# Tokens of k tiles 4 to 7 placed 128 bytes further on in their SBUF tile

## The chip, the cores and the metric

One Trainium2 chip; the kernel runs as one launch on one of its cores. The metric is the device time of that launch in microseconds. A run's time is compared with runs of the kernel before on the same chip.

## The reference

One layer of a bidirectional encoder on 256 tokens of width 2048, all in float32:

```python
h = rmsnorm(x)
q, k, v, u = split(h @ w_in)             # 1536 + 512 + 512 + 512 columns
a = rmsnorm(window_attention(q, k, v))   # 12 heads of 128, 4 kv heads, |t-s| <= 128, ALiBi, sink
f = rmsnorm(fourier_mix(u))              # per group: Re(DFT2 over positions and channels), a map
x = x + concat(a, f) @ w_out
gate, val = split(rmsnorm(x) @ w_up)     # 2 x 5504 columns
gate = depthwise_conv3(gate) + dw_b
x = x + (gelu(gate) * val) @ w_down
y = rmsnorm(x)
```

## The kernel before

**Numbers in two parts.** Each float32 matrix is split on the chip into a high part, which the reduced float32 type of TensorE (F32R) holds, and a low part, the rest. A product is three matmuls: high by high, high by low, low by high. ScalarE writes the high part (L170 for weights, L262 for tokens), VectorE subtracts to get the low one (L171, L263).

**The tokens.** Sixteen k tiles of 128 features each. Four SBUF tiles `hT0` to `hT3` hold four k tiles each; a k tile is 512 floats in every partition, 256 tokens of the high part and 256 of the low. So `hT1` holds k tiles 4 to 7. Behind the attention the same memory takes the normalised residual under the names `hU0` to `hU3` (`turn_x_out`).

**The weights.** They stream from HBM in units of 128 x 2048 floats (`raw`, three buffers) and are split into `parts` (three buffers of 2 x 2048 + 128 floats). `PLACES` says how many floats behind the start of its half each part begins: (0, 32) for "still", (16, 16) for "first", (0, 0) for "moving", (28, 28) for "product".

**Two kinds of matmul.** In `moving_weights` (L303 to L313) the tokens are the stationary operand and 512 columns of weights move: u, v, the output projection, late parts of the down projection. In `still_weights` (L315 to L325) a 128x128 block of weights is stationary and 256 tokens move; one tile of 128 output features takes 16 k tiles times three matmuls, 48 in all, all recorded under L322. There are 16 such tiles for q and k (`ps_q`, `ps_k`) and 86 for the up projection (`ps_gate`, `ps_val`), 102 together. Within a k tile the order is: high weights by high tokens, high weights by low tokens, low weights by high tokens.

**The order of the work.** It is written out by hand. u and v come first; then the q and k tiles, with the matmuls of attention and of the Fourier group put between them (`at(before, ...)`); then the output projection (L309 to L311); then the list of `ff_items`: gate and value tiles of features 0 to 7 back to back, then groups in which a product of the down projection (L1010 to L1012, 512 columns) stands behind every up tile but some, then late down products, the last six up tiles back to back, and the last down products. Each step splits the weights of the unit two ahead.

**The Fourier group.** After L505 ScalarE copies each of four groups out of PSUM into `yh` (L513, two buffers) and VectorE joins them into `y` (L518 to L522) one step later; the copy of the next group follows in the next step.

Of the kernel before, what the change touches and what calls it, by code (L numbers as in the profile page):

```python
# [8 lines left out]
F32 = mybir.dt.float32  # L9
F32R = mybir.dt.float32r  # L10
# [3 lines left out]
P = 128  # L14
D = 2048
S = 256
# [15 lines left out]
V_G1, V_G2, V_GA, V_GF, V_DW, V_DB, V_SINK = 0, 16, 32, 44, 48, 177, 220  # L32
# [15 lines left out]
N_U, N_V, N_QK = 0, 4, 8  # L48
# [35 lines left out]
def block_kernel(  # L84
# [21 lines left out]
    base = ctx.enter_context(tc.tile_pool(name="base", bufs=1))  # L106
# [4 lines left out]
    def f32(ap):  # L111
        return ap.bitcast(F32)

    def bank(pool, name):
        return pool.tile([P, 512], F32, tag=pool.name, name=name)


    units = [(w_in[i], 2048, "first" if i < N_QK else "still") for i in range(24)]
    units += [(w_out[i], 2048, "moving") for i in range(16)]
    n_front = len(units)  # L120
    items, up_index = ff_items(), {}
# [11 lines left out]
    raws, halves = {}, {}  # L133


    PLACES = {"still": (0, 32), "first": (16, 16), "moving": (0, 0), "product": (28, 28)}

    def parts_tile(name, place):
        t = wp.tile([P, 2 * 2048 + 128], F32R, tag="parts", name=name, bufs=3)
        oh, ol = PLACES[place]  # L140
        return t[:, oh : oh + 2048], t[:, 2048 + ol : 4096 + ol]

    def load(i, pieces=1):
        if i < len(units) and i not in raws:
            src, n, _ = units[i]
            raws[i] = wp.tile([P, 2048], F32, tag="raw", name=f"raw{i}", bufs=RAW)
            m = n // pieces
            for p in range(pieces):
                s = slice(p * m, (p + 1) * m)
                nc.sync.dma_start(raws[i][:, s], src[:, s])  # L150
                yield
# [28 lines left out]
    ph = pa.enter_context(tc.tile_pool(name="pa", bufs=1))  # L180

    hT = []
    vec = base.tile([P, V_N], F32, tag="vec", name="vec")
    xTc = [cat_pool.tile([P, 512], F32, tag="cat", name=f"xT{c}") for c in range(8)]
    chan = cat_pool.tile([P, 512], F32, tag="cat", name="chan")[:, 0 : 2 * P]
# [16 lines left out]
    first = load(0, 4)  # L202
# [50 lines left out]
    ps = bank(dn, "ps_warm")  # L253
# [3 lines left out]
    def vcol(o, n=1):  # L257
        return vec[:, o : o + n]

    def split_scaled(dst, src, g):  # L260

        nc.scalar.activation(dst[:, 0:S], src, AF.Copy, scale=g)  # L262
        nc.vector.scalar_tensor_tensor(  # L263
            dst[:, S : 2 * S], src, g, f32(dst[:, 0:S]), ALU.mult, ALU.subtract
        )
# [49 lines left out]
    def still_weights(hi, lo, ps, kk):  # L315


        for k in kk:
            h = hT[k // 4][:, k % 4, :]
            s = slice(k * P, (k + 1) * P)  # L320
            for n, (w, o) in enumerate([(hi, 0), (hi, S), (lo, 0)]):
                nc.tensor.matmul(  # L322
                    ps[:, 0:S], w[:, s], h[:, o : o + S],
                    start=k == 0 and n == 0, stop=k == NK - 1 and n == 2,
                )  # L325

    def hk(k):
        return hT[k // 4][:, k % 4, :]

    later = []  # L330

# [26 lines left out]


    for c in range(4):  # L360
        t = base.tile([P, 4, 512], F32R, tag=f"hT{c}", name=f"hT{c}")
        hT.append(t)
    ps_u = [bank(mm, f"ps_u{b}") for b in range(2)]
    for k in range(NK):
        c, q = k // 4, k % 4
        if q == 0:
            parts = split_parts(c, 4 if c < 2 else 2)
        split_scaled(hk(k), xTc[k // 2][:, (k % 2) * S : (k % 2 + 1) * S], vcol(V_G1 + k))
        next(parts, None)
        hi, lo = halves[c]  # L370
        for b in range(2):
            moving_weights(
                hi, lo, 512, [k], hk, b, ps_u[b], k == 0, k == NK - 1, q0=q
            )
        if q == 3:
            for _ in parts:
                pass
            del halves[c]
# [77 lines left out]
    held = {}  # L456
# [52 lines left out]


    def fourier_channels_copy(g):
        h = held["h", g] = ph.tile([P, S], F32, tag="tmp", name=f"yh{g}", bufs=2)
        nc.scalar.activation(h, held.pop(("y", g))[:, 0:S], AF.Copy)  # L513

    def fourier_channels_join(g):
# [30 lines left out]
    def fourier_channels_steps():  # L546
        for g in range(NG):
            i = 8 + g
            at(before, i, fourier_channels, g)
            at(beside, i, fourier_channels_copy, g)  # L550
            at(behind, i, fourier_channels_join, g)
            at(beside, i + 1, fourier_channels_out, g)
        at(before, 14, total, sq_f, "f")
        at(beside, 14, total_scale, "f", FW)
# [3 lines left out]
    for c in range(4):  # L558

        def work(hi, lo):  # L560
            for b in range(2):
                moving_weights(
                    hi, lo, 512, range(4 * c, 4 * c + 4), hk, b, ps_v[b], c == 0, c == 3
                )

        unit(N_V + c, work)
# [138 lines left out]
    for n, (kind, h) in enumerate(QK_ORDER):  # L705

        def work(hi, lo):
            ps = st["ps", kind, h] = bank(mm, f"ps_{kind}{h}")
            still_weights(hi, lo, ps, range(NK))

        unit(N_QK + n, work)
# [22 lines left out]
    def turn_x(c):  # L734
        turn_x_out(c, turn_x_in(c))
# [14 lines left out]
        return pss  # L750

    def turn_x_out(c, pss):
        t = base.tile([P, 4, 512], F32R, tag=f"hT{c}", name=f"hU{c}")
        for k4 in range(4):
            ps = pss[k4 // 2][:, k4 % 2 * S : (k4 % 2 + 1) * S]
            split_scaled(t[:, k4, :], ps, vcol(V_G2 + 4 * c + k4))
        hT2.append(t)

    at(before, N_OUT + 6, total, sq_a, "a")
# [2 lines left out]
    for n, (c, kq) in enumerate(OUT_ORDER):  # L762
        i = N_OUT + n

        def work(hi, lo):
            if kq == 0:
                ps_a[c] = [bank(mm, f"ps_a{c}{b}") for b in range(2)]
            if kq == 3:
                ps_a[c, "f"] = [bank(dn, f"ps_ff{c}{b}") for b in range(2)]
            ps = ps_a[c] if kq < 3 else ps_a[c, "f"]  # L770
            for b in range(2):
                moving_weights(
                    hi, lo, 512, range(4 * kq, 4 * kq + 4), cat.get, b, ps[b],
                    kq in (0, 3), kq in (2, 3),
                )

        unit(i, work)
        if kq >= 2:
            part = "a" if kq == 2 else "f"
            ps = ps_a[c] if kq < 3 else ps_a[c, "f"]  # L780
            last = c in added
            added.add(c)
            if n == len(OUT_ORDER) - 1:
                later.append(out_post(c, part, ps))
                continue

            at(behind if (c, kq) == (0, 2) else beside, i + 1, out_add, c, part, ps)
            if last:
                at(behind, i + 1, out_sums, c)
                at(before, i + 2, lambda c=c: st.update({("x", c): turn_x_in(c)}))  # L790
                at(beside, i + 2, lambda c=c: turn_x_out(c, st.pop(("x", c))))
# [180 lines left out]
    held = {(c, p): bank(dn, f"ps_{p}_{c}") for c in range(2) for p in ("P1", "N5")}  # L972
# [98 lines left out]
    for q in range(2):  # L1071
        kind, j = items[q]
        ps = bank(mm, f"ps_{kind}{j}")
        pair.append((ps, *halves.pop(n_front + q)))
        still_weights(*pair[q][1:], ps, range(12))
        if q == 0:
            ff_step(0)
            turn_x(3)
            hT[:] = hT2
    for ps, hi, lo in pair:  # L1080
        still_weights(hi, lo, ps, range(12, NK))
# [7 lines left out]
    for n, it in enumerate(items):  # L1089
# [8 lines left out]
        if it[0] in ("gate", "val"):  # L1098
            kind, j = it
            ps = bank(mm, f"ps_{kind}{j}")  # L1100
# [4 lines left out]
        if it[0] == "product":  # L1105
            kind, g, c, p = it
# [3 lines left out]
            else:  # L1110
                ps = bank(mm, f"ps_{p}{g}{c}")
# [4 lines left out]
        else:  # L1116
            kind, g, c = it
            hi, lo = halves.pop(up_index[n])
            ps = [bank(mm, f"ps_l{g}{c}{b}") for b in range(2)]
# [10 lines left out]
    i = up_index[n]  # L1130
# [145 lines left out]
```

## Time and profile before

| | |
|---|---|
| median of 3 runs | 959.62 us (959.04 to 959.85) |
| the profiled execution | 959.13 us, of which the span from first to last instruction 957.4 |
| TensorE, matmuls | 947.8 us busy, 99% of the span |
| TensorE, weight loads | 884.8 us, 92% |
| VectorE | 703.0 us, 73% |
| ScalarE | 510.5 us, 53% |
| HBM read | 208.65 MB, 220 GB/s over the span |
| mean granted TensorE clock | 0.997 |

How to read it: PE is a matmul, PEld a load of stationary weights, which overlaps it. Matmuls are pipelined, so the time of one (from its start to its end) is longer than the spacing of two. In the timeline, neighbours of one line and tile are merged into one row: start, time from the first start to the last end, count.

### The profile page before, as it was taken

The page shows a single profiled execution, that of the slowest core. Times are in us where ns is not written, and L with a number is a line of the kernel's source. Part 1 is how long each engine was busy: PE and PEld are TensorE (multiplying, and loading weights), DVE is VectorE, ACT ScalarE, POOL GpSimd, SP SyncE. Part 2 cuts the span into 40 slices and gives each one's busy share as a digit, 9 for nine tenths or more (in the row PEclk, how much of TensorE's full clock was granted, in tenths as well). Part 3 has the DMA queues.
Part 4 walks back from the last instruction along what each step waited for, and adds up shares of the span by engine and source line. Part 5 has one row for each costly group of instructions (what it writes and reads, how often), then busy time and mean ns, then how long its engine had stood idle before and what let it go on. Part 6 is the DMA issues. An engine that isn't in the chain of part 4 may idle for free.

```text
span 957.4 us, 15831 instructions
## 1 busy us (share of the span) xinstructions
PE 947.8 (99%) x6721; PEld 884.8 (92%) x6721; DVE 703.0 (73%) x822; ACT 510.5 (53%) x552; POOL 44.6 (5%) x59
## 2 busy tenths in 40 slices
PE   9999999999999999999999999999999999999996
PEld 7799999888899999999999999999999999998985
DVE  5658766666566667786888877987778879787664
ACT  6855655544453346555555555554555655553433
POOL 0000000000000000000000000000000000000003
PEclk9999999999999999999999999999999999999998
DMA  8954444455555676879688798777987786775542
GB/s 322 340 195 164 161 138 157 151 176 186 196 181 197 253 224 209 231 248 301 205 270 251 232 293 264 234 251 221 285 256 249 218 292 200 242 246 211 177 132 88
DMA packets 33558, 211.77 MB, mean 221 GB/s; under 512 B 3792, under 2 KB 4304, under 8 KB 9424
## 3 DMA queue, kind: packets, MB, share of 16 engines
q1 hardware_dynamic: 29744, 184.54, 52.8%
q0 software_dynamic: 3600, 26.22, 14.7%
q8 instruction: 52, 0.85, 0.3%
q14 instruction: 18, 0.15, 0.1%
q10 hardware_dynamic: 144, 0.01, 0.0%
HBM read 208.65 MB, written 2.10 MB: 220 GB/s over the span
## 4 chain that ended last, share of the span: by engine, by line
PE 96%; DMA 2%; ACT 0%; DVE 0%; issue 0%; POOL 0%; ACTq 0%; POOLq 0%; SPq 0%
PE ps_gate L322 25%; PE ps_val L322 25%; PE ps_q L322 7%; PE ps_P L1010 3%; PE ps_P L1011 3%; PE ps_P L1012 3%; PE ps_k L322 2%; PE ps_a L311 2%; PE ps_a L309 2%; PE ps_a L310 2%; PE ps_N L1010 2%; PE ps_N L1012 2%; PE ps_N L1011 2%; DMA raw<-in_w_in 2%; PE ps_l L309 2%; PE ps_l L310 2%
## 5 line engine op out<-in xcount | busy, mean ns | idle before, releaser
L171 DVE TENSOR_TENSOR parts<-raw,parts 128x2048 fp32r<-128x2048 f32 (+3 forms) x145 | 313.1, 2159 | 76.7 <-ACT parts L170 76.3
L170 ACT ACTIVATE parts<-raw 128x2048 fp32r<-128x2048 f32 (+3 forms) x144 | 262.4, 1823 | 170.4 <-PE ps_val L322 40.0
L322 PEld LDWEIGHTS ps_gate<-hU,parts 128*128 128x128 f32 x2064 | 242.6, 188 | 2.3
L322 PE MATMUL ps_gate<-hU,parts 128*128 128x256 f32 x2064 | 244.5, 277 | 0.0
L322 PEld LDWEIGHTS ps_val<-hU,parts 128*128 128x128 f32 x2064 | 242.1, 188 | 2.2
L322 PE MATMUL ps_val<-hU,parts 128*128 128x256 f32 x2064 | 244.1, 277 | 0.0
L322 PE MATMUL ps_q<-hT,parts 128*128 128x256 f32 x576 | 69.5, 279 | 0.0
L322 PEld LDWEIGHTS ps_q<-hT,parts 128*128 128x128 f32 x576 | 67.9, 188 | 0.0
L1011 PE MATMUL ps_P<-parts_P,op_P 128*128 128x512 f32 x128 | 49.8, 389 | 0.0
L1010 PE MATMUL ps_P<-parts_P,op_P 128*128 128x512 f32 x128 | 49.8, 389 | 0.0
L1012 PE MATMUL ps_P<-parts_P,op_P 128*128 128x512 f32 x128 | 49.8, 389 | 0.0
L906 ACT ACTIVATE parts_N<-sumw 128x2048 fp32r<-128x2048 f32 x16 | 30.7, 1917 | 35.7 <-PE ps_val L322 22.5
L907 DVE TENSOR_TENSOR parts_N<-sumw,parts_N 128x2048 fp32r<-128x2048 f32 x16 | 36.6, 2289 | 16.8 <-ACT parts_N L906 16.8
L309 PE MATMUL ps_a<-parts,cat 128*128 128x512 f32 x96 | 37.9, 395 | 0.0
L311 PE MATMUL ps_a<-parts,cat 128*128 128x512 f32 x96 | 37.5, 390 | 0.0
L310 PE MATMUL ps_a<-parts,cat 128*128 128x512 f32 x96 | 37.3, 389 | 0.0
L1010 PE MATMUL ps_N<-parts_N,op_N 128*128 128x512 f32 x96 | 37.3, 389 | 0.0
L1011 PE MATMUL ps_N<-parts_N,op_N 128*128 128x512 f32 x96 | 37.3, 389 | 0.0
L1012 PE MATMUL ps_N<-parts_N,op_N 128*128 128x512 f32 x96 | 37.3, 389 | 0.0
L804 DVE TENSOR_TENSOR fa_g<-ps_gate,r2b 128x256 f32<-128x256 f32 x43 | 18.1, 422 | 23.1 <-PE ps_gate L322 23.1
L1012 PEld LDWEIGHTS ps_P<-parts_P,op_P 128*128 128x128 f32 x128 | 24.0, 188 | 5.0
L906 ACT ACTIVATE parts_P<-sumw 128x2048 fp32r<-128x2048 f32 x8 | 15.3, 1917 | 23.1 <-PE ps_gate L322 13.2
(307 smaller groups left out, 1267.3 us busy)
## 6 DMA issues: line engine op xcount, KB each, us to landing
raw<-in_w_up SPq DMA_DIRECT2D x86, 1024.0 KB, 5.4
raw<-in_w_in SPq DMA_DIRECT2D x21, 1024.0 KB, 4.9
raw<-in_w_out SPq DMA_DIRECT2D x16, 1024.0 KB, 4.8
sumw<-in_w_down POOLq DMA_DIRECT2D x16, 1024.0 KB, 8.8
raw<-in_w_down_late SPq DMA_DIRECT2D x8, 1024.0 KB, 5.0
raw<-in_w_down_last SPq DMA_DIRECT2D x4, 768.0 KB, 4.3
raw<-in_w_in SPq DMA_DIRECT2D x8, 256.0 KB, 6.2
xs<-in_x SPq DMA_DIRECT2D x4, 512.0 KB, 10.1
```

The lines of the kernel that those rows point to most:

```text
L170: nc.scalar.activation(hi[:, s], raw[:, s], AF.Copy)
L171: nc.vector.tensor_tensor(lo[:, s], raw[:, s], f32(hi[:, s]), ALU.subtract)
L309: nc.tensor.matmul(ps, ah, wh, start=first and q == q0, stop=False)
L310: nc.tensor.matmul(ps, al, wh, start=False, stop=False)
L311: nc.tensor.matmul(ps, ah, wl, start=False, stop=last and q == q0 + len(kk) - 1)
L322: nc.tensor.matmul(ps[:, 0:S], w[:, s], h[:, o : o + S], start=k == 0 and n == 0, stop=k == NK - 1 and n == 2,)
L804: nc.vector.tensor_tensor(add, ps[:, 0:S], r2b, ALU.mult)
L906: nc.scalar.activation(hi, src, AF.Copy)
L907: nc.vector.tensor_tensor(lo, src, f32(hi), ALU.subtract)
L1010: nc.tensor.matmul(ps, o[:, 0, p, :], hi[:, s], start=first and p == 0, stop=False)
L1011: nc.tensor.matmul(ps, o[:, 1, p, :], hi[:, s], start=False, stop=False)
L1012: nc.tensor.matmul(ps, o[:, 0, p, :], lo[:, s], start=False, stop=last and p == 3)
```

## The change

The tile of k tiles 4 to 7 gets 128 floats more, and its contents begin 32 floats (128 bytes) further on; this holds for `hT1` and for `hU1`. The weights of u and v that are multiplied with these k tiles (units 1 and 5) move from place (16, 16) to (48, 48), also 128 bytes further. The weights of all other stages stay where they were in their tiles, so that in the 102 tiles of `still_weights` tokens and weights stand otherwise to each other at k tiles 4 to 7 than at the other twelve. All tiles behind `hT1` in SBUF begin 512 bytes later. To make room, `yh` has one buffer instead of two.

```diff
-    units = [(w_in[i], 2048, "first" if i < N_QK else "still") for i in range(24)]
+    first = ["first", "first_off", "first", "first"] * 2
+    units = [(w_in[i], 2048, first[i] if i < N_QK else "still") for i in range(24)]
...
-    PLACES = {"still": (0, 32), "first": (16, 16), "moving": (0, 0), "product": (28, 28)}
+    PLACES = {"still": (0, 32), "first": (16, 16), "first_off": (48, 48), "moving": (0, 0), "product": (28, 28)}
...
+    def tokens_tile(c, name):
+        o = 32 if c == 1 else 0
+        n = 2048 + (128 if c == 1 else 0)
+        t = base.tile([P, n], F32R, tag=f"hT{c}", name=f"{name}{c}")
+        return [t[:, o + q * 512 : o + (q + 1) * 512] for q in range(4)]
...
-            h = hT[k // 4][:, k % 4, :]
+            h = hT[k // 4][k % 4]
...
-        t = base.tile([P, 4, 512], F32R, tag=f"hT{c}", name=f"hT{c}")
-        hT.append(t)
+        hT.append(tokens_tile(c, "hT"))
...
-        h = held["h", g] = ph.tile([P, S], F32, tag="tmp", name=f"yh{g}", bufs=2)
+        h = held["h", g] = ph.tile([P, S], F32, tag="tmp", name=f"yh{g}", bufs=1)
...
-        t = base.tile([P, 4, 512], F32R, tag=f"hT{c}", name=f"hU{c}")
+        t = tokens_tile(c, "hU")
...
-            split_scaled(t[:, k4, :], ps, vcol(V_G2 + 4 * c + k4))
+            split_scaled(t[k4], ps, vcol(V_G2 + 4 * c + k4))
```

More of the change, by code (lines that the diff above doesn't have):

```diff
@@ L327, in hk @@
     def hk(k):
-        return hT[k // 4][:, k % 4, :]
+        return hT[k // 4][k % 4]
     later = []
```

## Prediction

> **What bounds the kernel now.** The page comes first: who is busy, and whose work ends last.
>
> ```profile
> span 957.4 us, 15831 instructions
> ...
> PE 947.8 (99%) x6721; PEld 884.8 (92%) x6721; DVE 703.0 (73%) x822; ACT 510.5 (53%) x552; POOL 44.6 (5%) x59
> ...
> PE 96%; DMA 2%; ACT 0%; DVE 0%; issue 0%; POOL 0%; ACTq 0%; POOLq 0%; SPq 0%
> ...
> L322 PE MATMUL ps_gate<-hU,parts 128*128 128x256 f32 x2064 | 244.5, 277 | 0.0
> ```
>
> TensorE is the chain (96%) and never idles in front of the gate matmuls (0.0). So nothing that other engines do sooner can help; only the spacing of one matmul behind the other can. The busy row hides that spacing, because matmuls overlap: 277 ns is from start to end of one. The spacing is read from windows that hold nearly nothing but matmuls of L322, as length over count.
>
> ```profile
> core 0: us, PE busy (x), PEclk, DMA share, GB/s
> 285.00:364.00 79.00, 79.00 (x667) 1.00 0.66 226
> 479.30:495.60 16.30, 16.30 (x146) 1.00 0.91 293
> 876.60:910.00 33.40, 33.40 (x282) 1.00 0.55 189
> ```
>
> The first and the third window give 118.4 ns for each matmul, the second 112 (with two from the edges in its count). All run at the full granted clock, and the quicker window has the busier DMA. The same instruction on the same shapes therefore has two spacings, and neither the clock nor DMA traffic makes the difference. The timeline of TensorE, which merges the 48 matmuls of one weight tile (16 k tiles, three matmuls each) into a row, shows where each spacing rules. Columns: start, time from the first start to the last end, line.
>
> ```profile
> 273.32 5.95 PE L322 MATMUL ps_gate<-hU,parts 128*128 128x256 f32 x48
> 279.11 5.87 PE L322 MATMUL ps_val<-hU,parts 128*128 128x256 f32 x48
> ...
> 364.71 5.87 PE L322 MATMUL ps_gate<-hU,parts 128*128 128x256 f32 x48
> 370.41 0.40 PE L1010 MATMUL ps_P<-parts_P,op_P 128*128 128x512 f32 x1
> ...
> 373.19 5.61 PE L322 MATMUL ps_val<-hU,parts 128*128 128x256 f32 x48
> 378.64 0.39 PE L1010 MATMUL ps_P<-parts_P,op_P 128*128 128x512 f32 x1
> ```
>
> ```profile
> 479.28 5.60 PE L322 MATMUL ps_gate<-hU,parts 128*128 128x256 f32 x48
> 484.72 5.60 PE L322 MATMUL ps_val<-hU,parts 128*128 128x256 f32 x48
> 490.16 5.60 PE L322 MATMUL ps_gate<-hU,parts 128*128 128x256 f32 x48
> 495.60 0.39 PE L1010 MATMUL ps_P<-parts_P,op_P 128*128 128x512 f32 x1
> ```
>
> ```profile
> 876.40 0.39 PE L311 MATMUL ps_l<-parts,act 128*128 128x512 f32 x1
> 876.63 5.87 PE L322 MATMUL ps_gate<-hU,parts 128*128 128x256 f32 x48
> ...
> 905.17 5.87 PE L322 MATMUL ps_val<-hU,parts 128*128 128x256 f32 x48
> 910.87 0.40 PE L309 MATMUL ps_l<-parts,act 128*128 128x512 f32 x1
> ```
>
> From 279.11 to 370.41 lie 16 tiles in a row: 91.30/16 = 5.706 us each, 118.9 ns for a matmul. From 479.28 to 495.60 lie three: 5.44 each, 113.3 ns. From 876.63 to 910.87 lie six: 5.707. I call the two the slow and the quick rhythm; they differ by 0.267 us a tile. The point for this change: a rhythm lasts. Over those 16 tiles nothing ends the slow one, though two weight buffers change places at each tile; the first product (370.41) ends it, and behind it all tiles up to the late down products are quick. In the projection of queries and keys other matmuls stand between the tiles, and either rhythm can follow:
>
> ```profile
> 75.60 5.96 PE L322 MATMUL ps_q<-hT,parts 128*128 128x256 f32 x48
> ...
> 82.10 5.87 PE L322 MATMUL ps_k<-hT,parts 128*128 128x256 f32 x48
> 87.81 0.60 PE L646 MATMUL ps_t<-ident,sc 128*128 128x128 f32 x4
> ...
> 88.96 5.63 PE L322 MATMUL ps_q<-hT,parts 128*128 128x256 f32 x48
> 94.42 0.40 PE L668 MATMUL ps_o<-pt,v_hi 128*128 128x256 f32 x2
> ...
> 159.16 5.87 PE L322 MATMUL ps_q<-hT,parts 128*128 128x256 f32 x48
> ```
>
> The tile at 82.10 took 5.71 to the next start (slow), the one at 88.96 took 5.46 (quick but for its first matmuls). Seven of the sixteen q and k tiles are slow: 75.60 is the first, 159.16 the last, and each such row is 5.87 or longer. By the page weight loads are busy for 92% of the span, beside the matmuls. So I suppose that the rhythm is a matter of where the load of the next weights stands against the stream of tokens, and that their addresses then count; no row shows it.
>
> **The change part by part.** *The tokens.* TensorE gets the same 6721 matmuls in the same order; no wait is added to it. Only the addresses at k tiles 4 to 7 move, by 32 floats, 128 bytes. In the built program the token tiles begin 96 bytes behind a multiple of 256, the weight tiles 32 bytes behind one; with the places (0, 32) the high halves of the weights lie 64 bytes before the tokens and the low halves 64 after, counted modulo 256 (that 256 is the step that counts is my assumption). A shift by 128 exchanges the two. So in each tile the pattern of distances turns over at k = 4 and turns back at k = 8: two disturbances in the middle of a tile, where until now there was none. I take it that they end the slow rhythm and leave the quick one alone. For the second half speaks that in the quick rhythm both distances already occur in each k tile (high, high, low) with no stall at either, and the turned pattern is made of the same two.
>
> What that saves: the slow tiles are seven of q and k; the first 36 matmuls of the first gate, with this row and its successor:
>
> ```profile
> 260.97 4.45 PE L322 MATMUL ps_gate<-hU,parts 128*128 128x256 f32 x36
> 265.26 1.04 PE L744 MATMUL ps_x<-ident,xs 128*128 128x128 f32 x8
> ```
>
> (4.29 us against 36 x 0.1133 = 4.08, so 0.21 too long); 17 from 273.32 to 370.41; and six at the end. (7 + 17 + 6) x 0.267 + 0.21 = 8.2 us. If the turn at k = 4 ends the slow rhythm, each fresh entry into it keeps four of its 16 k tiles: ten entries (seven of q and k, the first two gates, the gate at 876.63) x 0.067 = 0.7. The gain is 7.5 us. If it is the turn at k = 8, ten x 0.133 = 1.3 stays, and the gain is 6.9.
>
> *u and v.* Their weights at k tiles 4 to 7 move by the same 128 bytes as the tokens, so the distance within a matmul stays.
>
> ```profile
> L310 PE MATMUL ps_v<-parts,hT x32: 389/389/397, 30.2 to 55.9; 128*128 128x512 f32 x32
> ```
>
> Minimum and median are 389 ns, the longest 397. At the worst, 48 such matmuls of k tiles 4 to 7 (two stages of 24) lose 8 ns each, 0.4 us; as a gain there is nothing below the 389 that most already take. I take 0. The two turns into and out of those k tiles are one matmul each.
>
> *The Fourier copy.* Room for the longer tile comes from `yh`, one buffer for two: ScalarE's copy of a group now waits until VectorE has joined the group before.
>
> ```profile
> 69.23 0.16 DVE L522 COPY y<-yh 128x2 f32<-128x2 f32 x1
> ```
>
> ```profile
> 70.15 0.36 ACT L513 ACTIVATE yh<-ps_y 128x256 f32<-128x256 f32 x1
> ```
>
> The join ends at 69.39, the copy starts at 70.15: 0.76 us of cover, so 0. Were it gone, the wait would hold the split of a weight tile, which is queued behind the copy on ScalarE and which TensorE uses a unit later. The later start of ScalarE by some tens of ns may, though, shift into which rhythm a q or k tile falls: up to seven tiles either way, 1.9 us at most, and less where the turns end a slow one.
>
> The sum goes against the profiled execution: 959.13 - 7.5 = 951.6. The median of the three runs, 959.62, lies 0.5 above that execution, so I forecast 952.1.
>
> **The rivals.** *The quick tiles are thrown out.* The same turns could end the quick rhythm. Then the 71 tiles that are quick now (102 less 30 and most of the first gate) pay from k = 4 on: until k = 8, where the old pattern returns, 71 x 0.067 = 4.8 us, which gives 964.4; to the end of the tile, 71 x 0.2 = 14.2, so 973.8, since the product behind a tile starts the next one quick again. Its place is the stretch from 373 to 852, and it decides if a tile behind a product has a slow stretch at k = 4. For it: seven slow against nine quick among the q and k tiles show that a disturbance may leave either. Against it: a change of weight buffer, a change of PSUM bank and 0.91 of DMA time have not moved the quick tiles.
>
> *Nothing moves.* If addresses don't count, or count in steps of 128 bytes or less, the rhythms stay where they are: 959.6. It comes out the same if the slow rhythm outlives both turns. For it: the rows show that a rhythm survives everything but other matmuls in between, and none of them shows an effect of an address. The Trainium skill, "SBUF — State Buffer", section "Who interferes with whom", has this as a rule: TensorE reads moving and stationary operands through two independent ports and waits on no one, so by it the sum is 0 and the time 959.6. The two spacings of one instruction at one clock are not accounted for by that rule.
>
> **How the numbers follow.** Faster, 0.52: a quick rhythm that is made of both distances should stand, and a slow one that meets two disturbances in each tile has over 30 tiles to fall out, and stays out. Its own range is 950.9 (all 8.2 us and some of the entries) to 955 (half of the chains hold out longer). Nothing moves, 0.13. Quick tiles thrown out, 0.35, about half of it with a return at k = 8. The range goes from 950.9 to 965.0: that takes in the first two and the milder half of the third, and leaves out some 0.2. About 0.2%, 1.9 us, is what a measurement of this kernel can tell from no change; the three cases lie on the three sides of that bound.
>
> **What would show it.** Right: in the timeline the rows from 273 to 370 and behind 876 shrink from 5.87 to 5.60, and the count in a window such as the first rises from 667 to about 697; the rows behind products stay at 5.60; slow q and k tiles shrink to about 5.7. The forecast is wrong if rows behind products grow to 5.67 (k 4 to 7 alone) or 5.80 (to the end), or if the runs of 5.87 stand as they are. An idle time in front of L170 or L513 that now ends with VectorE would show the single buffer as a cost.

## The result

| | before | changed |
|---|---|---|
| median | 959.51 us (959.04 to 959.85, 4 runs) | 972.40 us (971.63 to 972.74, 4 runs) |
| ratio | | 1.0134, 95% interval 1.0116 to 1.0151 |
| profiled execution | 959.13 us, span 957.4 | 972.74 us, span 970.9 |

The change makes the kernel 12.9 us slower, where 7.5 us less had been forecast, and the time lies above the range. The granted clock is the same (0.997 and 0.998). The page of the changed kernel; L332 in it is L322 of before:

```profile
span 970.9 us, 15832 instructions
...
PE 960.4 (99%) x6721; PEld 894.4 (92%) x6721; DVE 703.4 (72%) x822; ACT 510.0 (53%) x552; POOL 44.6 (5%) x59
...
L332 PE MATMUL ps_gate<-hU,parts 128*128 128x256 f32 x2064 | 248.7, 279 | 0.0
```

The same 6721 matmuls, again with no idle time in front of the gate ones, are busy 12.6 us longer: what changed is the spacing. The timeline of TensorE at the places that the prediction read (start, time from the first start to the last end): first the back-to-back tiles and the tiles behind products, then the first of the six at the end, then the k tile and the q tile that started at 82.10 and 88.96 before.

```profile
281.05 5.81 PE L332 MATMUL ps_val<-hU,parts 128*128 128x256 f32 x48
286.70 5.81 PE L332 MATMUL ps_gate<-hU,parts 128*128 128x256 f32 x48
...
371.40 0.40 PE L1019 MATMUL ps_P<-parts_P,op_P 128*128 128x512 f32 x1
...
374.17 5.76 PE L332 MATMUL ps_val<-hU,parts 128*128 128x256 f32 x48
379.77 0.40 PE L1019 MATMUL ps_P<-parts_P,op_P 128*128 128x512 f32 x1
...
382.54 5.76 PE L332 MATMUL ps_gate<-hU,parts 128*128 128x256 f32 x48
388.14 0.40 PE L1019 MATMUL ps_N<-parts_N,op_N 128*128 128x512 f32 x1
...
390.92 5.76 PE L332 MATMUL ps_val<-hU,parts 128*128 128x256 f32 x48
```

```profile
890.53 5.82 PE L332 MATMUL ps_gate<-hU,parts 128*128 128x256 f32 x48
```

```profile
83.49 5.77 PE L332 MATMUL ps_k<-hT,parts 128*128 128x256 f32 x48
...
90.25 5.77 PE L332 MATMUL ps_q<-hT,parts 128*128 128x256 f32 x48
```

The slow rows did shrink, from 5.87 to 5.81: 16 tiles lie between 281.05 and 371.40, 90.35/16 = 5.647 us each against 5.706. But every quick row grew, from 5.60 to 5.76: from 374.17 to 379.77 are 5.60 us where a quick tile takes 5.44. The two sorts of tile now differ by 0.05 us only. The reason is seen inside one. Three windows within the tile at 390.92 (k 1 to 3, k 5 to 7, k 9 to 15), each with its group of matmuls; the last number but one is the mean length of one, which is 276 ns in a quick stretch:

```profile
L332 PE MATMUL ps_val<-hU,parts 128*128 128x256 f32 x10 | 1.3, 276 | 0.0
```

```profile
L332 PE MATMUL ps_val<-hU,parts 128*128 128x256 f32 x9 | 1.2, 276 | 0.0
```

```profile
L332 PE MATMUL ps_val<-hU,parts 128*128 128x256 f32 x21 | 2.7, 280 | 0.0
```

The tile starts quick, stays quick at k 4 to 7, where the tokens lie further on, and is slow behind the turn back. More closely, by the starts of the single matmuls in the trace: the ns from the first matmul of a k tile to the first of the next, for k = 0 to 15 (a bar at each turn, the start of the tile in us ahead).

```
before, 364.71, behind a tile     353 360 353 360 354 360 353 360 353 360 354 360 353 360 353 360
before, 381.36, behind a product  340 throughout
after,  286.70, behind a tile     354 360 353 360 | 348 340 340 340 | 352 360 353 360 354 360 353 360
after,  390.92, behind a product  352 340 340 340 | 357 340 340 340 | 351 360 354 360 353 360 353 360
```

340 is the quick rhythm (113.3 x 3), 353 and 360 by turns the slow one. Summed over all 102 tiles, what lies over 340 ns at each k:

```
                k 0 to 3   k 4 to 7   k 8 to 15     all
before            2.99       2.06       4.12       9.17 us
after             3.98       1.46      13.40      18.84 us
```

All 102 tiles are quick at k 5, 6 and 7, and all 102 are slow from k = 8 to 15. So 9.67 us of the loss lie in the tiles, 9.28 of them behind the turn back. A second part lies in the products, with their groups in the changed kernel and one of their three lines before:

```profile
L1020 PE MATMUL ps_P<-parts_P,op_P 128*128 128x512 f32 x128 | 50.8, 397 | 0.0
L1019 PE MATMUL ps_P<-parts_P,op_P 128*128 128x512 f32 x128 | 50.4, 394 | 0.0
L1021 PE MATMUL ps_P<-parts_P,op_P 128*128 128x512 f32 x128 | 49.6, 388 | 0.0
```

```profile
L1010 PE MATMUL ps_P<-parts_P,op_P 128*128 128x512 f32 x128 | 49.8, 389 | 0.0
```

Two of the three lines are longer. From start to start a product of 12 matmuls takes 2.77 us behind a slow tile (371.40 to 374.17) and 2.72 behind a quick one (378.64 before, with the next tile at 381.36): over all 672 such matmuls 155.31 us against 152.37, 2.94 more. With 1.03 in u (24.67 to 25.70), the sum is 13.6, against 13.5 more in the span. The part in u is nearly all idle time and not spacing: TensorE stands still there for 1.39 us, 0.92 of it until ScalarE has written a part of the weights (L171, up to 12.99), against 0.45 us before. The output projection, the late down products, v and attention take the same time within 0.1 us.

### The profile page after: what moved, and what is told of

Same layout as the page of the kernel before. It is cut to its first block, busy times and chain, and to the rows that moved or that the text cites. A ratio compares the mean times of both kernels' runs of the same rounds, so it can differ in the third digit from the quotient of the medians.

```text
span 970.9 us, 15832 instructions
## 1 busy us (share of the span) xinstructions
PE 960.4 (99%) x6721; PEld 894.4 (92%) x6721; DVE 703.4 (72%) x822; ACT 510.0 (53%) x552; POOL 44.6 (5%) x59
## 4 chain that ended last, share of the span: by engine, by line
PE 96%; DMA 2%; ACT 0%; DVE 0%; issue 0%; POOL 0%; ACTq 0%; POOLq 0%; SPq 0%
PE ps_gate L332 25%; PE ps_val L332 25%; PE ps_q L332 7%; PE ps_P L1020 3%; PE ps_P L1019 3%; PE ps_P L1021 3%; PE ps_N L1020 2%; PE ps_k L332 2%; PE ps_N L1019 2%; PE ps_a L319 2%; PE ps_a L321 2%; PE ps_a L320 2%; PE ps_N L1021 2%; DMA raw<-in_w_in 2%; PE ps_l L319 2%; PE ps_l L321 1%
## 5 line engine op out<-in xcount | busy, mean ns | idle before, releaser
L171 ACT ACTIVATE parts<-raw 128x2048 fp32r<-128x2048 f32 (+3 forms) x144 | 262.3, 1822 | 175.0 <-PE ps_val L332 40.3
L332 PE MATMUL ps_gate<-hU,parts 128*128 128x256 f32 x2064 | 248.7, 279 | 0.0
L332 PE MATMUL ps_val<-hU,parts 128*128 128x256 f32 x2064 | 248.7, 279 | 0.0
L332 PEld LDWEIGHTS ps_gate<-hU,parts 128*128 128x128 f32 x2064 | 246.3, 188 | 2.6
L332 PEld LDWEIGHTS ps_val<-hU,parts 128*128 128x128 f32 x2064 | 246.2, 188 | 2.5
L332 PE MATMUL ps_q<-hT,parts 128*128 128x256 f32 x576 | 70.0, 280 | 0.0
L332 PEld LDWEIGHTS ps_q<-hT,parts 128*128 128x128 f32 x576 | 68.3, 188 | 0.0
L813 DVE TENSOR_TENSOR fa_v<-ps_val,r2b 128x256 f32<-128x256 f32 x43 | 18.2, 423 | 16.7 <-PE ps_val L332 16.7
```

The source lines that it names most:

```text
L171: nc.scalar.activation(hi[:, s], raw[:, s], AF.Copy)
L332: nc.tensor.matmul(ps[:, 0:S], w[:, s], h[:, o : o + S], start=k == 0 and n == 0, stop=k == NK - 1 and n == 2,)
L813: nc.vector.tensor_tensor(add, ps[:, 0:S], r2b, ALU.mult)
```

## The experiments

Times are medians where several runs are named. "Excess" is what the 102 tiles take over 340 ns for each k tile; "products" is the time of the 672 matmuls of the down projection up to the next start (before: 9.17 and 152.37).

**One buffer for `yh`, and nothing else** (against the kernel before).

```diff
-        h = held["h", g] = ph.tile([P, S], F32, tag="tmp", name=f"yh{g}", bufs=2)
+        h = held["h", g] = ph.tile([P, S], F32, tag="tmp", name=f"yh{g}", bufs=1)
```

> The kernel before with one buffer for the Fourier copy, and nothing else of the change. Theory A (the turn back at k = 8 makes the loss): 959.5, rows behind products stay at 5.60, and only q and k tiles may change their rhythm, up to 1.9 us either way. Rival B (the single buffer costs part of the 12.9 us): 962 or more, with idle time in front of the weight splits that ends with VectorE.

959.37 us in one run, the kernel before 960.39 in seven on the same chip. Excess 9.18, products 152.37. In the changed kernel the line of the copy (durations, starts) now shows three semaphore events (one before) and no idle time that ends with VectorE:

```profile
L522 ACT ACTIVATE yh<-ps_y x4: 361/373/386, 58.5 to 77.4; 128x256 f32<-128x256 f32 x4
L522 ACTq EVENT_SEMAPHORE  x3: 17/17/17, 64.6 to 77.4; - x3
```

The buffer costs nothing, and the slow tiles stand where they stood.

**The distances turned in all k tiles, by the weights alone** (against before). In all k tiles the high halves now lie 64 bytes after the tokens modulo 256 and the low ones 64 before them; I call this the turned pattern, which the change makes at k 4 to 7 alone.

```diff
-    PLACES = {"still": (0, 32), ...}
+    PLACES = {"still": (32, 64), ...}
```

> The kernel before with the parts of all still weights 32 floats further on, (32, 64) for (0, 32), so that modulo 256 bytes the high half stands to the tokens everywhere as it does at k 4 to 7 in the changed kernel, with no turn anywhere. Theory A (these turned distances end the slow rhythm by themselves; only going back to the old ones starts it): nearly all 102 tiles at 5.44, 951.5. Rival C (it is the turns that disturb, and any constant distance holds either rhythm): 957.5 to 961.5, with slow and quick tiles mixed as before.

952.70 us (952.16 to 953.91, 4 runs) against 960.39 (959.54 to 960.64, 7 runs): ratio 0.9926, interval 0.9910 to 0.9943. It beats both kernels. Its page, and rows of its timeline from the back-to-back tiles and behind products:

```profile
span 950.6 us, 15831 instructions
...
L322 PE MATMUL ps_gate<-hU,parts 128*128 128x256 f32 x2064 | 241.7, 276 | 0.0
```

```profile
277.14 5.60 PE L322 MATMUL ps_val<-hU,parts 128*128 128x256 f32 x48
282.58 5.60 PE L322 MATMUL ps_gate<-hU,parts 128*128 128x256 f32 x48
```

```profile
366.91 5.62 PE L322 MATMUL ps_val<-hU,parts 128*128 128x256 f32 x48
```

Excess 2.15, products 152.64. From k = 3 on all 102 tiles are quick (344 ns at most at k = 3; behind a product 353, 341, then 340). The turned pattern by itself is thus never slow for long; in the changed kernel it is its end that costs.

**The distances turned by the tokens alone** (against before; u's and v's weights go along, `yh` with one buffer).

```diff
+    base.tile([P, 32], F32, tag="pad0", name="pad0")
...                                        # the four tiles hT0 to hT3
+    base.tile([P, 96], F32, tag="pad1", name="pad1")
...
-    PLACES = {..., "first": (16, 16), ...}
+    PLACES = {..., "first": (48, 48), ...}
```

> The kernel before with all tokens 128 bytes further on (and u's and v's weights with them, and one buffer for the Fourier copy): the same distances modulo 256 as with the still weights at (32, 64), by moving the other operand. Theory A: within 0.5 us of that run, 951.5. Theory D (absolute addresses of tokens or weights count, not the distance): the two runs differ.

961.05 us in one run, so not within half a microsecond of the kernel above. Excess 4.13: the tiles are quick here too, all 102 from k = 4 on, with a longer start behind a product (349, 357, 357, 344, then 340).

```profile
385.35 5.65 PE L322 MATMUL ps_val<-hU,parts 128*128 128x256 f32 x48
```

```profile
L1012 PE MATMUL ps_P<-parts_P,op_P 128*128 128x512 f32 x128 | 50.8, 397 | 0.0
```

But the products take 157.92 us, 5.3 more than with the turned weights, and all three of their lines are at 396 or 397 ns. Their own addresses modulo 256 are unchanged; what differs is where the tile in front of them left off. The remaining 1.4 us between the two runs lie in u (26.00 against 24.64). So the distance decides inside a tile. How the next stage runs goes with the place of the tokens: behind a quick tile a product takes 2.72 or 2.73 us with the tokens in their old place, whichever of the two places the weights have, and 2.82 with the tokens moved.

**A shift of 256 bytes instead of 128** (against the changed kernel).

```diff
-    PLACES = {..., "first_off": (48, 48), ...}
+    PLACES = {..., "first_off": (80, 80), ...}
...
-        o = 32 if c == 1 else 0
+        o = 64 if c == 1 else 0
```

> The changed kernel with 64 floats (256 bytes) for 32 at k tiles 4 to 7, and (80, 80) for u's and v's weights there. Theory A with a step of 256 bytes: as if nothing were shifted, 959.5, rows behind products 5.60. Rival E (any shift in mid-tile, or a step of 512 bytes and more): slow stretches behind k = 8 again, 965 or more.

959.20 us in one run; excess 9.18, products 152.37, tile by tile as before:

```profile
364.77 5.87 PE L332 MATMUL ps_gate<-hU,parts 128*128 128x256 f32 x48
...
373.25 5.62 PE L332 MATMUL ps_val<-hU,parts 128*128 128x256 f32 x48
```

A shift by 256 bytes is none. The other edits of the change (longer tile, other slices, later addresses behind it) cost nothing.

**k tiles 8 to 11 moved instead of 4 to 7** (against the changed kernel; units 2 and 6 of u and v go along).

```diff
-        o = 32 if c == 1 else 0
-        n = 2048 + (128 if c == 1 else 0)
+        o = 32 if c == 2 else 0
+        n = 2048 + (128 if c == 2 else 0)
```

> The changed kernel with k tiles 8 to 11 moved for 4 to 7 (and u's and v's weights for them). Theory A (the turn back starts the slow rhythm): behind a product a tile is quick up to k = 11 and slow only at 12 to 15, so each of some 70 such tiles is 0.067 us shorter than in the changed kernel: 972.4 - 4.7 = 967.7, with products as slow as there. Rival F (the turn into the moved k tiles starts it, or the whole tile suffers): no shorter than the changed kernel, 972.

968.27 us in one run, the kernel before 958.98. Three windows of the tile at 390.01, before the moved k tiles, in them and behind them:

```profile
L332 PE MATMUL ps_val<-hU,parts 128*128 128x256 f32 x21 | 2.5, 276 | 0.0
```

```profile
L332 PE MATMUL ps_val<-hU,parts 128*128 128x256 f32 x8 | 1.1, 276 | 0.0
```

```profile
L332 PE MATMUL ps_val<-hU,parts 128*128 128x256 f32 x10 | 1.4, 280 | 0.0
```

All 102 tiles are slow at k 12 to 15, where the excess is 6.61, and 102 quick at k 9 to 11. The loss begins where the old pattern comes back, wherever that is.

**k tiles 4 to 15 moved: no turn back inside a tile** (against before; `yh` with one buffer).

```diff
-    units = [(w_in[i], 2048, "first" if i < N_QK else "still") for i in range(24)]
+    units = [(w_in[i], 2048, ("first_off" if i % 4 else "first") if i < N_QK else "still") for i in range(24)]
...
-    PLACES = {..., "first": (16, 16), ...}
+    PLACES = {..., "first": (16, 16), "first_off": (48, 48), ...}
...
+        if c == 1:                         # ahead of hT1
+            base.tile([P, 32], F32, tag="pad0", name="pad0")
...                                        # behind hT3
+    base.tile([P, 96], F32, tag="pad1", name="pad1")
```

> k tiles 4 to 15 moved (and u's and v's weights for them): the turn back falls on the border to the next tile. Theory A: every tile is quick from k = 5 to 15; the tiles back to back begin slow at k 0 to 3, those behind products don't. Still tiles 5 us shorter than before the change; products, which begin from the turned distance as with all tokens moved, 5.5 us longer: 959 to 962. Rival F: slow stretches behind k = 4, 968 or more.

964.09 us in one run, 2 us over what was expected. From k = 5 to 14 all 102 tiles are quick, and k 8 to 15 has an excess of 0.06 us instead of 13.40. Two windows of the tile at 386.05 (k 1 to 3, k 5 to 15), and the products:

```profile
L322 PE MATMUL ps_val<-hU,parts 128*128 128x256 f32 x10 | 1.3, 280 | 0.0
```

```profile
L322 PE MATMUL ps_val<-hU,parts 128*128 128x256 f32 x33 | 3.9, 276 | 0.0
```

```profile
L1013 PE MATMUL ps_P<-parts_P,op_P 128*128 128x512 f32 x128 | 50.8, 397 | 0.0
```

The products came as expected, 5.5 us longer: at 157.92, as with all tokens moved, since now the last k tile lies further on. The miss is in the tiles, which were to save 5 us and saved 1.4: behind such a product a tile starts slow, which the expectation had ruled out, and stays so up to the turn at k = 4. That costs 6.35 us at k 0 to 3, where it was 2.99. Another 0.66 us lies in v (22.86 against 22.20).

**The mirror image: the turned pattern everywhere but at k 4 to 7** (against the changed kernel).

```diff
-    PLACES = {"still": (0, 32), ...}
+    PLACES = {"still": (32, 64), ...}
```

> The changed kernel with still weights at (32, 64): now k tiles 4 to 7 have the old distances and the other twelve the turned ones. Theory A: the mirror image; slow at k 4 to 7 in every tile, quick again from 8 or 9 to the end and into the next tile: 102 tiles x 0.08 us on top of 952.7, 961. Rival F (it is the second disturbance of a tile that starts the slow rhythm, whatever the distances): quick at 4 to 7, slow from 8 on, 970 or more.

960.45 us in one run. Windows of the tile at 386.56 at k 1 to 3, k 5 to 7 and k 9 to 15:

```profile
L332 PE MATMUL ps_val<-hU,parts 128*128 128x256 f32 x9 | 1.2, 276 | 0.0
```

```profile
L332 PE MATMUL ps_val<-hU,parts 128*128 128x256 f32 x9 | 1.2, 280 | 0.0
```

```profile
L332 PE MATMUL ps_val<-hU,parts 128*128 128x256 f32 x20 | 2.4, 276 | 0.0
```

Spacings: 353 341 340 340 | 352 360 353 360 | 347 341 340 throughout. All 102 tiles are slow at k 4 to 7, now the four with the old pattern, and all are quick from k = 9. Both turns act at each place where they were put, each always in its own direction.

**u's and v's weights left in place** (against the changed kernel).

```diff
-    PLACES = {..., "first_off": (48, 48), ...}
+    PLACES = {..., "first_off": (16, 16), ...}
```

> The changed kernel with u's and v's weights of k tiles 4 to 7 left at (16, 16). Theory A: only u's and v's matmuls can change, by at most 0.4 us each way: 972.4 give or take 0.8. Rival G (moving u's and v's weights is itself part of the loss): 971 or less.

972.22 us in one run; excess 18.84 and products 155.30, as in the changed kernel; u 25.07 us, v 22.35 (changed kernel 25.70 and 22.21).

```profile
L332 PE MATMUL ps_gate<-hU,parts 128*128 128x256 f32 x2064 | 248.7, 279 | 0.0
```

The move of u's and v's weights is no part of the loss, and leaving it out gains nothing. u itself took from 24.6 to 26.0 us over all these kernels without following any edit, so the 1.03 above is not put down to the change.

**Both halves 64 bytes before the tokens, then both 64 after them** (each against the kernel before).

```diff
-    PLACES = {"still": (0, 32), ...}
+    PLACES = {"still": (0, 0), ...}     # the first of the two kernels
+    PLACES = {"still": (32, 32), ...}   # the second
```

> The kernel before with both halves of the still weights at 0: modulo 256 bytes every load of weights stands 64 bytes before the tokens, as two of three do in the kernel before. Theory H (this distance is the one that keeps a slow rhythm alive; the other ends it): slow tiles at least as many as before, 959 to 980. Theory I (a change of distance within the k tile is needed for the slow rhythm): all tiles quick, 951 to 953.

> Both halves at 32: every load stands 64 bytes behind the tokens, as two of three do at the turned distances. Theory H: quick from nearly every entry, 951 to 953, like the run with (32, 64). Theory I: the same. If slow tiles stay, more than 955, it takes both distances in the order high, high, low to end the slow rhythm, and neither theory holds.

975.43 and 969.64 us in one run each, the kernel before 959.71. With both before the tokens, a tile that follows a tile and one that follows a product:

```profile
286.31 5.82 PE L322 MATMUL ps_gate<-hU,parts 128*128 128x256 f32 x48
```

```profile
390.74 5.82 PE L322 MATMUL ps_val<-hU,parts 128*128 128x256 f32 x48
```

With both after the tokens, the tiles back to back up to the first product are quick (first row) and those behind products slow (the others):

```profile
283.79 5.60 PE L322 MATMUL ps_gate<-hU,parts 128*128 128x256 f32 x48
```

```profile
368.12 5.82 PE L322 MATMUL ps_val<-hU,parts 128*128 128x256 f32 x48
376.55 5.81 PE L322 MATMUL ps_gate<-hU,parts 128*128 128x256 f32 x48
```

The slow rhythm is another one here, 353 or 354 ns in each k tile. With both before the tokens it rules in 99 of 102 tiles (excess 21.91), with both after them in 72 (16.38). So neither distance is the bad one by itself, and neither of the two theories in these expectations holds: one distance throughout does no better than the old pattern. Of the four arrangements only the turned one, in which two matmuls of each k tile have weights after the tokens and the third before them, has the quick rhythm alone. The old one is its mirror and has both.

## Why the prediction was wrong

**Right: what bounds the kernel, and that addresses count.** TensorE's spacing is nearly all that moved (12.6 of the 13.6 us), and a shift of 128 bytes moves it while one of 256 doesn't. The assumption that 256 is the step is shown by the kernel with 256 bytes (959.20). The rule quoted from the Trainium skill, "SBUF — State Buffer", section "Who interferes with whom", by which TensorE waits on no one and the time would have stayed, gave the wrong time here: the same instructions took 952.70 and 975.43 us with nothing but `PLACES` for "still" changed. Whether what they lose is a wait at a port is not shown.

**Right: the turn at k = 4 ends the slow rhythm.** It did so in each tile that came to it slow (0.03 us of excess at k 5 to 7 in all, where there was 1.56). Each of the 102 tiles pays 7 to 17 ns at the turn, 1.43 us in all; so of k 4 to 7 only 0.60 us is won.

**Wrong: "end the slow rhythm and leave the quick one alone".** This is the step that failed. I treated the two turns as two disturbances of one sort. They are opposite: into the turned pattern every tile comes out quick, back into the old one every tile comes out slow, 102 of 102 in the changed kernel, with k 8 to 11 moved and in the mirror image. That cost 9.28 us at k 8 to 15, and took with it the gain that was booked there: instead of 30 slow tiles falling into the quick rhythm, 71 quick ones fell out of it. The support for the step was that the quick rhythm holds both distances in each k tile already. So it does, but that doesn't say which of them the two high matmuls of a k tile have and which the low one, and the pair (0, 32) against (32, 64) shows that this is what matters.

**Not foreseen: what the tile does to its successor.** A tile that ends slow hands on its rhythm. The 21 tiles that stand directly behind another in the two back-to-back stretches start slow again, each of them, and cost 1.40 us at k 0 to 3 as before, in place of the "stays out" of the forecast. The 0.99 us that k 0 to 3 lost beyond that lie with tiles that had been quick: 0.63 in the first k tiles behind products (352 ns for 340), 0.40 in the six tiles that follow another one between 480 and 760 us. And each product behind a slow tile takes 0.05 us longer, 2.94 in all. The prediction gave products no term.

**The rival.** "The quick tiles are thrown out" had the right sign and its larger price, 14.2 us to the end of the tile, was near, but it names the wrong turn: it was to decide by a slow stretch from k = 4 on, where all tiles are quick, and the loss begins at k = 8, where the rival's milder form let the old pattern end it. 71 tiles were to pay; in fact all 102 are slow at k 8 to 15, 13.40 us, of which 4.12 were there before. That the two numbers lie close is chance. It was right that a product starts the next tile quick. The rows behind products, which I had named as the sign of a wrong forecast at 5.67 or 5.80, came to 5.76: slow for eight k tiles instead of four or twelve.

**u, v and `yh` at nothing.** Right for the two moves: the single buffer alone changed nothing (959.37), and the changed kernel without the move of u's and v's weights took as long as with it (972.22). The 1.03 us more in u came nearly all from waiting, which no term of the prediction covers.

**What stays open.** That the arrangement of the two distances decides is shown; why is not. The supposition that it is a matter of where the next weights' load stands against the stream of tokens fits, but no run tests it. For the still weights only 64 bytes before and after the tokens were tried, so other distances are open. The products have two rhythms of their own: from start to start 226 or 227 ns behind a quick tile of the kernel before, 225, 231 and 237 by turns behind a slow one. With the tokens moved they are in the slow one too, behind quick tiles, after a start of 260, 246 and 234. Why is open; moving their weights was not tried.

## What to carry to other kernels

Where one engine is the whole chain, measure the spacing of its instructions tile by tile: the same matmul may have two, and which one rules can depend on where both operands lie modulo 256 bytes and on what ran before. A change of address in the middle of a stream is two changes, in and back, and they needn't act alike: try the new arrangement throughout before cutting it into pieces; here the turned pattern in all k tiles gained 7.7 us and in four of them lost 12.9. And look at the instructions behind the ones that were touched: how one stage ends can set the rhythm of the next.

## What the runs showed of the hardware

That, with the same instructions, an arrangement of addresses can have two lasting rhythms, only the quick one, or nearly only a slow one: per k tile of three matmuls 340 ns or 353 and 360 by turns for the places (0, 32), 340 alone for (32, 64), 340 or 353.3 for (32, 32), almost only 353.3 (the mean of 353 and 354) for (0, 0), at one granted clock of 0.997 to 0.998. And that matmuls of another shape run differently by what stood before them, with their own addresses the same modulo 256: a product takes 2.72 us behind a quick tile, 2.77 behind a slow one, and 2.82 behind a quick one whose last tokens lay 128 bytes further on (152.37, 155.31 and 157.92 us over 56 of them).
